# A two-layer hybrid backbone: who issues the stores of normalised tokens, and how many tiles of a SwiGLU begin with the first half

## The chip, the cores and the metric

One core of one Trainium2 chip. The metric is the device time of one execution in microseconds. Before the change it was 2889.73 us in the median of 3 runs (2886.65 to 2902.56).

## The reference

512 tokens of 1024 features go through two layers: 256 latent tokens and 256 context tokens. Each layer is a SwiGLU of half weight, a mixer of three branches (grouped attention, RWKV-7 and neighbourhood attention) and a second SwiGLU. Each of these three parts is modulated by a conditioning vector and closed by a layer norm:

```python
def post_norm(x, y, g, b):
    return layer_norm(ALPHA * x + y, g, b)

def swiglu(u, wi, wo):
    gate, up = jnp.split(u @ wi, 2, axis=-1)
    return (jax.nn.silu(gate) * up) @ wo

for l in range(DEPTH):
    x = post_norm(x, 0.5 * m_x[2] * swiglu(modulate(x, m_x[0], m_x[1]), ffn1_wi[l], ffn1_wo[l]), ...)
    ctx = post_norm(ctx, 0.5 * m_c[2] * swiglu(modulate(ctx, m_c[0], m_c[1]), ffn1_wi[l], ffn1_wo[l]), ...)
    y_x, y_c = hybrid_mixer(modulate(x, m_x[3], m_x[4]), modulate(ctx, m_c[3], m_c[4]), ...)
    x = post_norm(x, m_x[5] * y_x, ...)
    if not last:
        ctx = post_norm(ctx, m_c[5] * y_c, ...)
        ctx = post_norm(ctx, 0.5 * m_c[8] * swiglu(modulate(ctx, m_c[6], m_c[7]), ffn2_wi[l], ffn2_wo[l]), ...)
    x = post_norm(x, 0.5 * m_x[8] * swiglu(modulate(x, m_x[6], m_x[7]), ffn2_wi[l], ffn2_wo[l]), ...)
```

D_MODEL is 1024, D_FF is 2816, all in float32. In the last layer the context is dropped after the mixer's keys and values, so the last SwiGLU has latent tokens alone.

## The kernel before, in words

Everything lies transposed: features on the 128 partitions, tokens along a row of 512, of which the first 256 (`LAT`, "the first half") are latent tokens and the last 256 (`CTX`, "the second half") context. A D of 1024 is KD = 8 tiles, an FF of 2816 is KF = 22 tiles. A float32 product is made of three TensorE products: each operand is split into a high and a low part (`uh`/`ul` for the tokens, `whi`/`wlo` for a weight), and `gemm` adds high by high, high by low and low by high (L330 to L332).

A weight comes by `wload` (L307 to L325): SP issues a load into `raw` (L312; three buffers), ScalarE copies the high part (L320), VectorE subtracts (L321), which frees the buffer. High and low parts have two buffers each, unless the caller hands over tiles to hold them (`hold`): then a weight is split in two halves of 512 (`whh`/`whl` in a SwiGLU, `wG` in the mixer).

A SwiGLU (`ffn`, L462) runs over the 22 tiles of FF: a product with the gate weight (`ps_fg`), one with the up weight (`ps_fu`), silu on ScalarE into `sg` (L496), the product of the two on VectorE. Six banks are there for these products, two for each tile. Where both halves are present, the first `early` tiles are made by halves: first their products with the tokens of the first half, then those with the second half, since the second half's normalised tokens come later. The tiles from `early` on take all 512 tokens at once. Then follow eight output tiles (`ps_o`), the last of them by halves.

A layer norm stands between any two parts, for each half by itself. `ln_stats` (L408) makes the mean, the centred `z`, squares `sq` on ScalarE (L420), their sum on TensorE (`ps_ss`, L424), a small sum on VectorE, its power -1/2 on GpSimd (`rs`, L428), and spreads it on TensorE (`ps_bc`, L431). `ln_norm` (L434) multiplies z by it (L440) and modulates z into the next part's `uh`/`ul` (L351, L336, L337). In a second loop GpSimd applies gain and bias (`xn`, 128x256, L447, two buffers), and SP stores each xn in DRAM (`xd`, L450), from where the next part's residual reads it. Five norms have a next part, four of both halves and one of the first half alone: 72 stores of 128 KB. The sixth norm's eight stores are the output `out_y`.

The mixer begins with RWKV (`rwkv`, L903): four products of `ps_first` for both halves; the first two use weights that were split ahead (`ready`), the other two hold theirs in `wG` tiles. Their memory is where the SwiGLU's working tiles lay, xn among them. Behind them come gate products (`ps_gate`, L847 to L849) that fill gaps, and projections with weights of their own (L602, high part `phi`).

Each engine runs its instructions in one fixed order. A scheduler sets these orders when the kernel is built, by priorities and its own costs; SP's order is also that of its loads and stores. A transfer waits on the issuing engine for its data and for a free buffer, and what stands behind it there waits too.

Of the kernel before, what the change touches and what calls it, by code (L numbers as in the profile page):

```python
# [112 lines left out]
class Program:  # L113
# [320 lines left out]
    def ln_norm(self, l, ln, h, nxt, dst, bc, res=None):  # L434


        nc, z = self.nc, self.z
        for k in range(KD):
            with (self.tc.issue_after(res.ins) if res is not None and k >= 3 else nullcontext()):
                nc.vector.tensor_tensor(out=z[k][:, h], in0=z[k][:, h], in1=bc, op=ALU.mult)  # L440
                if nxt is not None:
                    self.modulate(k, h, z[k][:, h], *nxt)
        for k in range(KD):
            xn = self.tmp.tile([P, SEQ], F32, tag="xn", name="xn", bufs=2 if nxt is not None else 4)
            lg, lb = [self.lng[:, l, ln, i, k:k + 1] for i in range(2)]
            if nxt is not None:
                nc.gpsimd.tensor_scalar(out=xn, in0=z[k][:, h], scalar1=lg, scalar2=lb, op0=ALU.mult, op1=ALU.add)  # L447
            else:
                nc.scalar.activation(out=xn, in_=z[k][:, h], func=AF.Identity, scale=lg, bias=lb)
            nc.sync.dma_start(out=dst[k][:, h], in_=xn)  # L450

    def norm_dst(self, l, ln, nxt, final=None):
        if nxt is not None:
# [8 lines left out]
    def ffn(self, l, which, halves, nxt_fn, every, final=None, then=()):  # L462
        nc = self.nc
# [4 lines left out]
        with ExitStack() as ctx:  # L468
# [7 lines left out]
            two = len(halves) == 2  # L476
# [27 lines left out]
            def banks():  # L504
                return [self.bank("mm", [P, NT], n) for n in ("ps_fg", "ps_fu")]


            early = 2 if two else 0
            ps = [banks() for _ in range(early)]
            ready, self.ready = self.ready, []  # L510
            ws = [m == 0 and ready or load(m, True) for m in range(early)]
# [15 lines left out]
            nxt = nxt_fn()  # L527
            dst = self.norm_dst(l, ln, nxt, final)
# [1127 lines left out]
```

## Time and profile before

| | |
|---|---|
| runs | 2886.65, 2889.73, 2902.56 us |
| profiled execution, its own time | 2899.91 us |
| its span | 2898.1 us |
| granted TensorE clock, mean | 0.956 of full speed |
| busy, TensorE / VectorE / ScalarE / GpSimd | 2721.6 / 1715.2 / 1062.7 / 308.2 us |
| DMA | 379.74 MB in 207615 packets, none of them issued by GpSimd |

The busy times are those of one execution, and the span is the stretch that its trace covers; the 1.8 us around it are not in the trace. TensorE's granted clock is a share of its full speed: 2.4 GHz, with 1.2 GHz as the other level. In a timeline a row is one instruction, or several of a kind (xN), on an engine (PE is TensorE, DVE VectorE, ACT ScalarE, POOL GpSimd; SPq is SP's queue of DMA issues), with its start and its duration; brackets hold the engine's idle time before it and what ended that.

### The profile page before, as it was taken

The numbers are of one execution on the slowest core, as the hardware profiler recorded it, in microseconds if no ns is written. First come the engines' busy times: TensorE is split into PE (matmuls) and PEld (weight loads), VectorE is DVE, ScalarE is ACT, GpSimd is POOL, SyncE is SP. The second block draws the span as 40 slices with busy tenths as digits, with TensorE's granted clock in tenths as the row PEclk, the third lists the DMA queues.
The fourth block names the chain that finished last, engine by engine and source line by source line (L and its number), as shares of the span: only waits on it lengthen the run. The fifth ranks groups of instructions, "written<-read, shape, count | busy, mean of one in ns | idle before, by whom it ended". The sixth has DMA issues, their size and how long they took to land. (4 is left out here: it accounts for less than half of the span.)

```text
span 2898.1 us, 48420 instructions
## 1 busy us (share of the span) xinstructions
PE 2721.6 (94%) x19654; PEld 2218.8 (77%) x19654; DVE 1715.2 (59%) x2855; ACT 1062.7 (37%) x1928; POOL 308.2 (11%) x306
## 2 busy tenths in 40 slices
PE   7999998898899899999999999999898998898998
PEld 5788887676667676797888888888776777777998
DVE  4667345767652457657762476633578775386654
ACT  3222234333322346342222332322443443374443
POOL 0000022111100101220000100001221110022000
PEclk8999999999999999989999999999899999898998
DMA  7655342221133532436553465433332223544654
GB/s 281 203 179 176 105 126 92 76 70 48 53 89 119 153 114 87 146 117 197 178 164 108 126 200 181 135 102 116 112 114 64 62 71 101 164 129 143 218 178 146
DMA packets 207615, 379.74 MB, mean 131 GB/s; under 512 B 80032, under 2 KB 110368, under 8 KB 207392
## 3 DMA queue, kind: packets, MB, share of 16 engines
q1 hardware_dynamic: 207392, 376.65, 41.7%
q8 instruction: 154, 2.52, 0.4%
q14 instruction: 69, 0.57, 0.1%
HBM read 342.50 MB, written 33.03 MB: 130 GB/s over the span
## 5 line engine op out<-in xcount | busy, mean ns | idle before, releaser
L320 ACT ACTIVATE whi<-raw 128x1024 fp32r<-128x1024 f32 (+1 forms) x399 | 415.2, 1041 | 1117.6 <-PE ps_o L331 298.1
L321 DVE TENSOR_TENSOR wlo<-raw,whi 128x1024 fp32r<-128x1024 f32 (+1 forms) x399 | 499.2, 1252 | 499.1 <-ACT whi L320 493.0
L847 PE MATMUL ps_gate<-uh,whi 128*128 128x512 f32 (+1 forms) x672 | 266.8, 397 | 5.0 <-ACT fg L853 3.1
L330 PE MATMUL ps_o<-hh,whi 128*128 128x512 f32 (+1 forms) x770 | 270.8, 352 | 0.0
L253 DVE SCALAR_TENSOR_TENSOR acc<-araw,cs,acc 128x1024 f32<-128x1024 f32 x210 | 260.6, 1280 | 15.5 <-DMA araw<-in_w_ada 15.3
L332 PE MATMUL ps_o<-hh,wlo 128*128 128x512 f32 (+1 forms) x770 | 267.5, 347 | 0.0
L331 PE MATMUL ps_o<-hl,whi 128*128 128x512 f32 (+1 forms) x770 | 265.6, 345 | 0.0
L330 PE MATMUL ps_fg<-uh,whi 128*128 128x512 f32 (+1 forms) x704 | 256.3, 364 | 7.8 <-ACT uh L336 4.1
L332 PE MATMUL ps_fu<-uh,wlo 128*128 128x512 f32 (+1 forms) x704 | 252.8, 359 | 4.4 <-DVE wlo L321 4.4
L332 PE MATMUL ps_fg<-uh,wlo 128*128 128x512 f32 (+1 forms) x704 | 254.1, 361 | 2.3 <-DVE wlo L321 2.3
L331 PE MATMUL ps_fg<-ul,whi 128*128 128x512 f32 (+1 forms) x704 | 253.4, 360 | 0.1
L330 PE MATMUL ps_fu<-uh,whi 128*128 128x512 f32 (+1 forms) x704 | 251.9, 358 | 0.9 <-ACT whi L320 0.9
L331 PE MATMUL ps_fu<-ul,whi 128*128 128x512 f32 (+1 forms) x704 | 251.5, 357 | 0.0
L849 PE MATMUL ps_gate<-uh,wlo 128*128 128x512 f32 (+1 forms) x672 | 242.9, 361 | 1.1 <-DVE wlo L321 1.1
L848 PE MATMUL ps_gate<-ul,whi 128*128 128x512 f32 (+1 forms) x672 | 242.5, 361 | 0.0
L330 PEld LDWEIGHTS ps_fg<-uh,whi 128*128 128x128 f32 x704 | 135.4, 192 | 38.9 <-ACT whi L320 12.0
L332 PEld LDWEIGHTS ps_o<-hh,wlo 128*128 128x128 f32 x770 | 144.6, 188 | 20.2
L847 PEld LDWEIGHTS ps_gate<-uh,whi 128*128 128x128 f32 x672 | 131.6, 196 | 36.9 <-issue 7.2
L331 PEld LDWEIGHTS ps_o<-hl,whi 128*128 128x128 f32 x770 | 144.5, 188 | 19.5
L330 PEld LDWEIGHTS ps_o<-hh,whi 128*128 128x128 f32 x770 | 144.8, 188 | 19.0 <-ACT whi L320 1.7
L332 PEld LDWEIGHTS ps_fu<-uh,wlo 128*128 128x128 f32 x704 | 134.4, 191 | 26.0 <-DVE wlo L321 7.3
L332 PEld LDWEIGHTS ps_fg<-uh,wlo 128*128 128x128 f32 x704 | 135.1, 192 | 22.8 <-DVE wlo L321 3.3
(299 smaller groups left out, 5169.6 us busy)
## 6 DMA issues: line engine op xcount, KB each, us to landing
raw<-in_ffn_wi SPq DMA_DIRECT2D x176, 512.0 KB, 3.6
araw<-in_w_ada SPq DMA_DIRECT2D x144, 512.0 KB, 3.9
raw<-in_w_in SPq DMA_DIRECT2D x92, 512.0 KB, 3.6
raw<-in_ffn_wo SPq DMA_DIRECT2D x70, 448.0 KB, 3.3
raw<-in_ffn_wo SPq DMA_DIRECT2D x35, 512.0 KB, 3.5
pd<-fg SPq DMA_DIRECT2D x52, 256.0 KB, 2.0
raw<-in_w_branch SPq DMA_DIRECT2D x24, 512.0 KB, 3.8
raw<-in_w_in SPq DMA_DIRECT2D x44, 256.0 KB, 2.7
```

The lines of the kernel that those rows point to most:

```text
L253: nc.vector.scalar_tensor_tensor(out=a, in0=raw, scalar=c, in1=a, op0=ALU.mult, op1=ALU.add)
L320: nc.scalar.activation(out=hi[:, :m], in_=r, func=AF.Copy)
L321: self.lo = nc.vector.tensor_tensor(out=lo[:, :m], in0=r, in1=hi[:, :m].bitcast(F32), op=ALU.subtract)
L330: nc.tensor.matmul(pt, wh, xh[k], start=first and k == 0, stop=False)
L331: nc.tensor.matmul(pt, wh, xl[k], start=False, stop=False)
L332: nc.tensor.matmul(pt, wl, xh[k], start=False, stop=last and k == n - 1)
L847: nc.tensor.matmul(pt, wh, xh, start=k == 0, stop=False)
L848: nc.tensor.matmul(pt, wh, xl, start=False, stop=False)
L849: nc.tensor.matmul(pt, wl, xh, start=False, stop=k == KD - 1)
```

## The change

GpSimd issues the stores of xn where a next part follows; the output's stores stay on SP. A SwiGLU with two halves makes three tiles by halves instead of two, so the third tile's weights are held in split tiles too.

```diff
@@ ln_norm @@
             else:
                 nc.scalar.activation(out=xn, in_=z[k][:, h], func=AF.Identity, scale=lg, bias=lb)
-            nc.sync.dma_start(out=dst[k][:, h], in_=xn)
+            (nc.sync if nxt is None else nc.gpsimd).dma_start(out=dst[k][:, h], in_=xn)
@@ ffn @@
-            early = 2 if two else 0
+            early = 3 if two else 0
```

GpSimd's order from the first SwiGLU's norm to the mixer, before: the first half's xn, the second half's rs (`L428`), the second half's xn.

```order
L428 TENSOR_TENSOR rs<-rs,mhalf 128x2
L447 TENSOR_SCALAR xn<-z,c_lngb 128x256 x2
L908 MEMSET shp 128x2 x2
L1284 MEMSET R 128x256
L1285 MEMSET R 128x16
L447 TENSOR_SCALAR xn<-z,c_lngb 128x256 x6
L428 TENSOR_TENSOR rs<-rs,mhalf 128x2
L447 TENSOR_SCALAR xn<-z,c_lngb 128x256 x8
```

And now the end of the same stretch (the first half's last xn, and the first of the second half):

```order
L447 TENSOR_SCALAR xn<-z,c_lngb 128x256
L450 DMA xd_0_2334<-xn 128x256
L428 TENSOR_TENSOR rs<-rs,mhalf 128x2
L447 TENSOR_SCALAR xn<-z,c_lngb 128x256
L450 DMA xd_0_2334<-xn 128x256
```

Each of the 72 xn has its store right behind it, and the second half's rs comes behind eight xn and eight stores.

SP's order at the same place (`raw` are weights, those of L602 for the projections with `phi`; c_, lora and g_ are small constants):

```order
-L312 DMA raw<-in_w_in 128x1024 x3
-L450 DMA xd_0_2278<-xn 128x256 x2
-L312 DMA raw<-in_w_in 128x1024
-L450 DMA xd_0_2278<-xn 128x256 x2
+L312 DMA raw<-in_w_in 128x1024 x4
...
-L602 DMA raw<-in_w_in 128x512
-L450 DMA xd_0_2278<-xn 128x256 x2
-L1063 DMA g_4156<-in_lora 128x128
-L602 DMA raw<-in_w_in 128x512
-L450 DMA xd_0_2278<-xn 128x256 x4
-L312 DMA raw<-in_w_in 128x1024
-L450 DMA xd_0_2278<-xn 128x256 x4
-L312 DMA raw<-in_w_in 128x1024
```

All sixteen stores are gone from it; what stays are the loads, in their old order but for the small constants, which now stand ahead of both loads of L602.

TensorE's order at the end of this place, before: five gate products (`ps_gate`), then the first product with a held weight (`wG`).

```order
L847 MATMUL ps_gate_3638<-uh_2260,whi_3641 128x512
L848 MATMUL ps_gate_3638<-ul_2268,whi_3641 128x512
L849 MATMUL ps_gate_3638<-uh_2260,wlo_3642 128x512
L847 MATMUL ps_gate_3638<-uh_2261,whi_3641 128x512
L848 MATMUL ps_gate_3638<-ul_2269,whi_3641 128x512
L330 MATMUL ps_first_3380<-uh_2260,wG_3382 128x256
```

And now the last five of nine:

```order
L848 MATMUL ps_gate_3694<-ul_2325,whi_3697 128x512
L849 MATMUL ps_gate_3694<-uh_2317,wlo_3698 128x512
L847 MATMUL ps_gate_3694<-uh_2318,whi_3697 128x512
L848 MATMUL ps_gate_3694<-ul_2326,whi_3697 128x512
L849 MATMUL ps_gate_3694<-uh_2318,wlo_3698 128x512
L330 MATMUL ps_first_3436<-uh_2316,wG_3438 128x256
```

Four gate products have moved ahead of the first one with wG. On ScalarE phi stands behind two squares of the second half and ahead of six, where there were five and three.

## Rows read from the trace of the kernel before

**Rows 1.** Windows by stage; columns: stretch, length, busy us by engine, TensorE clock, DMA share, GB/s
```profile
400.00:480.00 80.00, 69.75 (x462) 63.14 (x462) 41.32 (x81) 38.46 (x75) 16.95 (x24) 0.91 0.37 113
1230.00:1290.00 60.00, 59.19 (x426) 57.83 (x426) 27.59 (x66) 25.50 (x57) 16.45 (x25) 0.86 0.26 82
2020.00:2090.00 70.00, 58.98 (x405) 55.06 (x404) 37.92 (x77) 34.36 (x70) 16.73 (x24) 0.85 0.37 117
```

**Rows 2.** Waits of SP's queue: line, releaser, us in total, times, longest us
```profile
SPq L450 <- POOL xn L447: 106.5, 54, 8.8
```

**Rows 3.** Tile xn: duration ns min/median/max; waits in us, times; landing us
```profile
L447 POOL TENSOR_SCALAR xn<-z,c_lngb x72: 552/556/1838, 425.6 to 2686.9; 128x256 f32<-128x256 f32 x72
L450 SPq DMA_DIRECT2D xd<-xn x72: 319/320/1299, 426.2 to 2687.4; - x72
...
  DMA xd<-xn: 29.2, 18
...
DMA to landing us min/median/max: 1.7/1.7/5.0
```

**Rows 4.** Lines of GpSimd by form: busy us, mean ns | idle before, releasers
```profile
L428 POOL TENSOR_TENSOR rs<-rs,mhalf 128x2 f32<-128x2 f32 x10 | 7.8, 781 | 95.3 <-DVE rs L427 95.3
```

**Rows 5.** Chain of waits, 2036 to 2080 us: start, duration, what
```profile
2063.54 1.45 POOL xn L447
...
2066.88 0.57 POOL xn L447
...
2072.38 1.72 DMA xd<-xn
```

**Rows 6.** Timeline of SP's queue at the first SwiGLU's norm: start, duration, instruction
```profile
435.40 0.37 SPq L602 DMA_DIRECT2D raw<-in_w_in  x1
```

**Rows 7.** Timeline of VectorE, same place
```profile
430.82 1.22 DVE L321 TENSOR_TENSOR wlo<-raw,whi 128x1024 fp32r<-128x1024 f32 x1
```

**Rows 8.** Timeline of ScalarE, same place; in brackets the idle time before, releaser
```profile
439.23 0.63 ACT L336 ACTIVATE phi<-raw 128x512 fp32r<-128x512 f32 x1 [3.18 <-DMA raw<-in_w_in]
...
459.57 1.67 ACT L320 ACTIVATE wG<-raw 128x512 fp32r<-128x512 f32 x3 [2.96 <-DMA xd<-xn]
```

**Rows 9.** Waits of TensorE, 420 to 480 us
```profile
PE ps_first L330 <- ACT wG L320: 2.4, 1, 2.4
PE ps_ss L424 <- ACT sq L420: 1.8, 1, 1.8
```

**Rows 10.** Timeline of GpSimd, 425 to 461 us
```profile
425.59 2.38 POOL L447 TENSOR_SCALAR xn<-z,c_lngb 128x256 f32<-128x256 f32 x2 [1.05 <-DVE z L440]
...
443.22 0.71 POOL L428 TENSOR_TENSOR rs<-rs,mhalf 128x2 f32<-128x2 f32 x1 [6.77 <-DVE rs L427]
445.29 1.09 POOL L447 TENSOR_SCALAR xn<-z,c_lngb 128x256 f32<-128x256 f32 x2 [1.37 <-DVE z L440]
```

**Rows 11.** Timeline of TensorE, 1289 to 1296 us: halves, then whole tiles
```profile
1289.80 0.28 PE L332 MATMUL ps_fu<-uh,whl 128*128 128x256 f32 x1
...
1292.04 0.40 PE L330 MATMUL ps_fg<-uh,whi 128*128 128x512 f32 x1
...
1295.92 0.39 PE L332 MATMUL ps_fg<-uh,wlo 128*128 128x512 f32 x1
```

**Rows 12.** Waits of TensorE, 2030 to 2090 us
```profile
PE ps_ss L424 <- ACT sq L420: 3.4, 1, 3.4
...
PE ps_first L330 <- ACT wG L320: 2.0, 1, 2.0
```

**Rows 13.** Timeline of GpSimd at the same norm of the second layer
```profile
2060.33 1.09 POOL L447 TENSOR_SCALAR xn<-z,c_lngb 128x256 f32<-128x256 f32 x2 [1.37 <-DVE z L440]
```

**Rows 14.** Timeline of ScalarE at the second layer's first SwiGLU
```profile
1654.95 0.63 ACT L320 ACTIVATE whh<-raw 128x512 fp32r<-128x512 f32 x1 [1.84 <-DMA raw<-in_ffn_wi]
```

**Rows 15.** Timeline of SP's queue at the last SwiGLU
```profile
2678.45 9.32 SPq L450 DMA_DIRECT2D xd<-xn  x8
```

**Rows 16.** Timeline of ScalarE at the last SwiGLU
```profile
2692.50 1.06 ACT L320 ACTIVATE whi<-raw 128x1024 fp32r<-128x1024 f32 x1 [1.39 <-PE ps_fg L331]
```

## The prediction

> **What bounds the kernel now.** I read the shares of busy time first (table above): TensorE is busy nearly all the time. A change that touches only GpSimd and SP can therefore pay only where TensorE stands still, so the second view is busy time by stage. Around the joints between a SwiGLU and the mixer TensorE is busy for 69.75 of 80 us and 58.98 of 70 us, at a granted clock of 0.91 and 0.85; at the joint from the first layer's mixer to its second SwiGLU it is busy for 59.19 of 60 us, so there is nearly nothing to win there [rows 1]. The third view is what SP's queue waits for: 54 of the 72 stores wait for their normalised token, 106.5 us in all [rows 2]. Every load queued behind such a store waits too, and that is what the move can free. The fourth view is the tile of normalised tokens, xn: GpSimd makes one in 0.56 us (median), at worst in 1.84 us; SP issues a store in 0.32 us and it lands after 1.7 us (medians); and GpSimd itself waits 29.2 us, 18 times, for a store to land, as there are two buffers [rows 3].
>
> **What moves.** All 72 stores of xn go from SP to GpSimd, where each stands behind its own xn; the eight stores of the final output stay on SP. GpSimd is not scarce, but its order is strict: between the first half's and the second half's tokens stands the rs of the second half's statistics, and it now stands behind eight issues more.
>
> **The unknown price c** is what one issue costs GpSimd. The trace has no transfer issued by GpSimd. From below it is SP's 0.32 us [rows 3]; from above I take 1.84 us, the slowest xn. Between them lies GpSimd's operation with next to no data, rs on 128x2, at 0.78 us mean [rows 4]. An issue touches no tile of data either, so it should stand near that row rather than at either end; I take 1.0 us, a little above it, and keep 0.32 and 1.84 for the range. The landing I leave at 1.7 us.
>
> With two buffers a round of two xn takes either xn, issue and landing (0.56 + c + 1.7), or two xn and two issues (1.12 + 2c), whichever is longer. At c = 1.0 that is 3.26 us. The round that binds today is 3.34 us (2063.54 to 2066.88 [rows 5]), so the rhythm stays. Eight tokens take three rounds, two xn with issue, and a landing: 3 x 3.26 + 3.12 + 1.7 = 14.6 us. At 0.32 it is 11.2 us, at 1.84 it is 20.9 us.
>
> By the Trainium skill ("DMA: Bandwidth & Descriptors", section "Anatomy of one DMA — SWDGE (gpsimd) path") a transfer issued by GpSimd takes about 2.0 us plus its bytes over 436 GB/s; for 128 KB that is an estimate of 2.3 us, where the SP-issued row has 1.7. By the page a group of eight would be four times 0.6 us longer, 2.4 us, and the sum below some 7 us higher, near 2893; no row of before can show it, and it stays inside no change.
>
> **Joint 1 (first SwiGLU to mixer, 425 to 462 us).** The load of a projection weight is issued at 435.40, behind stores, though its buffer was free at 430.82 + 1.22 = 432.04 [rows 6, 7]. ScalarE stands 3.18 us at phi for it, with three of the eight squares of the second half behind phi [rows 8], and TensorE waits 1.8 us for those squares [rows 9]. Without the stores the load goes out 3.4 us earlier. Phi moves ahead in ScalarE's order (behind two squares instead of five), so some of this stays; from the 1.8 us of TensorE and the 3.2 us of ScalarE I take 2.4. The rs is then at 440.8 instead of 443.22, and the first xn of this half at 442.9 instead of 445.29 [rows 10]. GpSimd is free for it: the first half's tokens begin at 425.59 and their last issue ends 14.6 - 1.7 later, at 438.5.
> The end of this joint is set by the last store: ScalarE's wG waits 2.96 us until it has landed, 459.57 [rows 8], and TensorE waits 2.4 us for wG [rows 9]. Now: 442.9 + 14.6 + 0.5 (half a chance of one xn slowed by 1.1 us) = 458.0, so 1.5 us earlier. Four more gate products stand ahead of the first product with wG, at 0.228 us each [rows 11], work that came after the wait: 0.9 us. Joint 1: **-2.4 us**.
>
> **Joint 2 (second layer, same code).** TensorE waits 3.4 us for squares here [rows 12]; I take 3.9 for the gain of the second half's chain, as the load is held longer. First xn of that half: 2060.3 [rows 13] - 3.9 = 2056.4; last landing 2056.4 + 15.1 = 2071.5 against 2072.38 + 1.72 = 2074.10 [rows 5]; with the gate products **-3.4 us**.
>
> **Starts of the SwiGLUs.** A tile's 48 products (gate and up, 8 tiles of D, three each) split into halves go from 0.228 us to two times 0.118 us (2.24 us for 19, 3.88 us for 17 [rows 11]): 48 x 0.008 = 0.36 us, in three SwiGLUs **+1.1 us**. What it would cover, a wait for the second half's norm, hardly exists: of 60 us 59.19 are busy [rows 1]. At the start of the second layer ScalarE stands 1.84 us at a held weight whose load left SP behind two stores [rows 14] and, behind it, the first half's modulation, for which TensorE waits. That load now leaves when its buffer is free, and no store holds the next ones: I count three quarters of the 1.84, **-1.4 us**. Three tiles take all six banks, so the fourth waits for the first tile's silu; that has the 11 us of the other two tiles' second half to finish in.
>
> **Joint 3 (last mixer to last SwiGLU, one half).** SP issues the eight stores in 9.32 us from 2678.45, one landing per round hidden by late tokens, and the last is down at about 2689.1 [rows 15]. On GpSimd, from an xn's 0.56 us before the first issue: 2677.9 + 14.6 = 2692.5, 3.4 us later. The first silu waits for it, and the third tile's weight split stands behind that silu with 1.39 us to spare [rows 16]: **+2.0 us**.
>
> Sum: -2.4 - 3.4 - 1.4 + 1.1 + 2.0 = **-4.1 us**, against the profiled execution's own 2899.9 us (span 2898.1). That execution lies 10 us over the median of the runs shown, 2889.73; the terms are differences, so I set them against the median: **2886 us**. A measurement of this kernel can tell about 0.5%, 14.5 us, from no change.
>
> **Rival one, slower: GpSimd is shut out while it issues.** The bound for it is in the trace: an xn takes 1.84 us in place of 0.56 when VectorE is at work beside it [rows 3]; one of 1.45 us stands in joint 2's chain [rows 5]. If every issue costs that, two xn and two issues are the round, 4.8 us, and eight tokens take 20.9 us. Joints 1, 2 and 3 end 6.3 us later each (+18.9). The first half's issues then last till 425.6 + 20.9 - 1.7 = 444.8 in joint 1, past the rs due at 440.8, and as far past it in joint 2: +4 to 5 us each. Two SwiGLU starts pass silu's deadline by some 3 us each. With the -4.1: about +30 us, **2919 us**. It decides from c = 1.2 us (sum zero) and is told from no change from about 1.5 us. For it speaks that VectorE is at work for half of joint 1's stretch, 41.32 of 80 us [rows 1]; against it, that the median of the 72 xn is at the low end, 0.56 us.
> The Trainium skill warns of this ("SBUF — State Buffer", the box "The 'DVE blocks DMA' trap (SWDGE)"): GpSimd writes the descriptors of its own transfers through a port shared with VectorE, and it advises SP's or ScalarE's queue instead. The same page's "Who interferes with whom" has two-operand operations bar only GpSimd's reads, by which the issue would be spared; the row shows reads barred and no issue.
>
> **Rival two, faster: the issue is as cheap as SP's.** At 0.32 us eight tokens take 11.2 us, and the stores cease to set the joints' ends. Then TensorE's own waits are the cap: 1.8 + 2.4 + 0.9 in joint 1 [rows 9], 3.4 + 2.0 + 0.9 in joint 2 [rows 12], joint 3 even, -1.8 at the second layer's start, +1.1: -12 us. With fewer stops the clock may also stay up: 9% of 80 us and 15% of 70 us, 17.7 us in all, are lost to it [rows 1]; a third of that is 6. **2872 us**.
>
> **Rival three, nothing happens:** the load that phi needs is bound by its buffer and the transfer, not by SP's queue, and the third tile covers a wait that isn't there. Then the eight tokens of joints 1 and 2 begin where they do now and end 0.9 and 1.3 us later, less 0.9 us of gate products each; with +1.1 and +2.0 that is about +3 us, **2893 us**.
>
> **Chances.** Forecast 0.40 and rival three 0.19 lie within 0.5%; rival one beyond 0.5% 0.23, for the price is unknown and the slope above 1.2 us is steep (some 4.6 us per tenth); rival two beyond 0.5% 0.18. The range goes from 2868 (rival two with a little more clock) to 2911 (rival one at about 1.65 us); some 0.06 lie below and 0.13 above.
>
> **What would show it.** Right: transfers of GpSimd in a queue of their own, about 1 us of GpSimd between one xn and the next, rounds of 3.3 us; phi's wait under 1.5 us, TensorE's wait for squares gone in both joints; wG released by the last store at 458 and 2071 plus the shift so far; the last SwiGLU's first silu 3 us later. Wrong: rounds of over 4 us, or a landing over 2.5 us; rs waiting behind the first half's issues; TensorE's waits for wG grown; or a granted clock that moves more than 0.01 over the span, which would outweigh every term here.

## The result and the profile after

The change makes the kernel slower: 2912.85 us in the median of 7 runs (2907.58 to 2916.63) against 2888.38 us before (7 runs as well, 2886.65 to 2902.56), a ratio of 1.0069 with a 95% interval of 1.0054 to 1.0084. The forecast was 2886 us with a range up to 2911. The profiled execution of the changed kernel took 2916.6 us (span 2914.9, mean granted clock 0.955), that of before 2899.9 (span 2898.1, 0.956); the two traces differ by 16.8 us, the medians by 24.5.

First the tile xn in the changed kernel (min/median/max in ns; waits in us, times; landing in us), which answers to [rows 3].

```profile
L447 POOL TENSOR_SCALAR xn<-z,c_lngb x72: 544/557/2670, 425.4 to 2704.7; 128x256 f32<-128x256 f32 x72
L450 POOL DMA_DIRECT2D xd<-xn x72: 587/587/747, 426.3 to 2705.5; - x72
...
  DMA xd<-xn: 11.8, 14
...
  ACT wG L320: 10.7, 2
...
  ACT L496: 7.1, 2
  ACT sg L496: 4.1, 1
...
DMA to landing us min/median/max: 1.7/2.1/5.3
```

An issue by GpSimd takes 0.59 us, nearly always the same, where SP's took 0.32. A store lands after 2.1 us where it took 1.7; both run from the start of the issue, and from its end the medians are 1.47 and 1.40 us, so most of the difference is the longer issue itself. GpSimd waits less for landings, 11.8 us instead of 29.2, but 42.8 us of issues now stand between its tokens. And what waits for the last store of a norm waits longer: wG 10.7 us in two places (5.5 before), silu, or the load of its table, in three SwiGLUs 11.2 us (0.9 in one before).

GpSimd's timeline in joint 1 shows what each token costs now; it answers to [rows 10].

```profile
425.43 0.56 POOL L447 TENSOR_SCALAR xn<-z,c_lngb 128x256 f32<-128x256 f32 x1 [1.05 <-DVE z L440]
...
430.21 0.59 POOL L450 DMA_DIRECT2D xd<-xn  x1 [0.30 <-POOL xn L447]
433.69 0.80 POOL L447 TENSOR_SCALAR xn<-z,c_lngb 128x256 f32<-128x256 f32 x1 [2.88 <-DMA xd<-xn]
...
441.49 0.59 POOL L450 DMA_DIRECT2D xd<-xn  x1 [0.30 <-POOL xn L447]
442.10 0.73 POOL L428 TENSOR_TENSOR rs<-rs,mhalf 128x2 f32<-128x2 f32 x1
444.14 0.56 POOL L447 TENSOR_SCALAR xn<-z,c_lngb 128x256 f32<-128x256 f32 x1 [1.31 <-DVE z L440]
...
458.40 0.59 POOL L450 DMA_DIRECT2D xd<-xn  x1 [0.30 <-POOL xn L447]
```

Behind each xn stand 0.30 us until its end is known, 0.59 us of issue and the next xn: 1.45 us at best. The first half's tokens run from 425.43 to 442.08; 2.88 us of that is a wait for a store of 428.18 that landed only after 5.3 us. And the second half's rs, which stands behind them, starts at 442.10, without a gap. The second half's tokens then take from 444.14 to 458.99. ScalarE's timeline at the same place ([rows 8] before):

```profile
435.42 0.64 ACT L336 ACTIVATE phi<-raw 128x512 fp32r<-128x512 f32 x1 [0.73 <-DMA raw<-in_w_in]
435.96 1.93 ACT L420 ACTIVATE sq<-z 128x256 f32<-128x256 f32 x6
...
460.62 0.63 ACT L320 ACTIVATE wG<-raw 128x512 fp32r<-128x512 f32 x1 [5.40 <-DMA xd<-xn]
```

Phi's wait has shrunk from 3.18 to 0.73 us and the eight squares are done at 437.9, as forecast. But the gain stops there: rs comes 4.2 us after the squares, and wG begins at 460.62, later than before (459.57). TensorE's waits, 420 to 480 us ([rows 9] before), say the same: the wait for squares is gone, one of 3.0 us for rs stands in its place, and the one for wG has grown from 2.4 to 4.0.

```profile
PE ps_first L330 <- ACT wG L320: 4.0, 1, 4.0
PE ps_bc L431 <- POOL rs L428: 3.5, 2, 3.0
```

The second loss is at the first layer's second SwiGLU. SP's queue there:

```profile
1301.35 0.81 SPq L242 DMA_DIRECT2D araw<-in_w_ada  x2
1302.27 0.37 SPq L312 DMA_DIRECT2D raw<-in_ffn_wi  x1
1306.49 0.33 SPq L242 DMA_DIRECT2D araw<-in_w_ada  x1
1306.87 0.90 SPq L356 DMA_DIRECT2D xr<-xd  x2
1309.47 17.78 SPq L242 DMA_DIRECT2D araw<-in_w_ada  x6
1328.10 0.33 SPq L312 DMA_DIRECT2D raw<-in_ffn_wi  x1
```

These araw are background work: weights of the next modulations, each load followed by 2.5 us of additions on VectorE (L253). Their first load waits until the last store of xn has landed and goes out at 1301.35, since its tile lies where xn lay. Then six more follow in a row, 17.78 us, before the fifth tile's second weight is loaded at 1328.10. What TensorE meets is on VectorE: the fourth tile's second `wlo` stands behind seven such pieces of additions, the first at 1305.05, and starts at 1326.82.

```profile
1326.82 1.22 DVE L321 TENSOR_TENSOR wlo<-raw,whi 128x1024 fp32r<-128x1024 f32 x1
```

The fifth tile's first `whi`, on ScalarE, stands behind a copy that waits for VectorE too. TensorE waits there as follows, first 1245 to 1350 us, then at the start of the second layer, 1640 to 1745 us, behind a product of the background itself.

```profile
PE ps_fu L332 <- DVE wlo L321: 4.3, 1, 4.3
PE ps_fg L330 <- ACT whi L320: 3.4, 1, 3.4
```

```profile
PE ps_ada L258 <- DVE acc L253: 7.7, 1, 7.7
```

At the last SwiGLU the first silu (with the load of its table) waits 5.84 us for the last store:

```profile
2707.89 1.28 ACT L496 ACT_TABLE_LOAD   x1 [5.84 <-DMA xd<-xn]
```

Busy time by stage answers to [rows 1]. The places are those of before, shifted by the lag so far: next to nothing was won where TensorE stood still.

```profile
400.00:480.00 80.00, 68.13 (x456) 62.08 (x455) 41.45 (x80) 38.03 (x75) 25.02 (x40) 0.89 0.35 114
1240.00:1300.00 60.00, 59.17 (x427) 57.80 (x426) 27.78 (x67) 23.48 (x57) 28.91 (x41) 0.86 0.28 93
2040.00:2110.00 70.00, 59.32 (x417) 54.72 (x417) 37.75 (x77) 35.65 (x72) 24.42 (x39) 0.90 0.36 117
```

How far each part is behind is seen from instructions that both traces have. The lag is the start in the changed kernel less that in the kernel before.

| instruction (start before) | changed | first part alone | second part alone |
|---|---|---|---|
| rs, first half, first norm (423.83) | -0.2 | -3.2 | -0.7 |
| first small rs of the mixer, L396 (481.69): end of joint 1 | +1.3 | -3.3 | +1.4 |
| rs, first half, mixer's norm (1250.68) | +10.2 | -1.2 | +5.8 |
| sixth silu of the second SwiGLU (1336.47) | +17.9 | +3.4 | +6.8 |
| rs, first half, its norm (1645.33) | +18.1 | +3.1 | +6.9 |
| sixth silu of the second layer (1730.05) | +18.9 | -1.7 | +7.4 |
| rs, first half, its norm (2037.25) | +18.9 | -1.7 | +7.4 |
| fifth shp of the mixer, L894 (2095.88): end of joint 2 | +16.3 | -4.2 | +6.3 |
| rs of the last mixer's norm (2675.78) | +13.4 | -5.8 | +9.0 |
| last rs (2888.78) | +16.5 | -2.2 | +6.5 |

Joint 1 costs 1.5 us, the second SwiGLU's start 7.7, the second layer's start 0.7, joint 2 gives 2.6, the last SwiGLU costs 3.1: 10.4 us of the 16.5. The rest lies in the mixers (+8.9 and -2.8). There the order of TensorE's instructions is that of before, and a second trace of the same changed kernel has +2.0 instead of +8.9 in the first mixer. The granted clock from 520 to 560 us is 1.00 before and 0.87 in the changed kernel, but 0.87 in that second trace too, so it doesn't tell the two apart. I count none of it for the change; what it is stays open.

A lag holds both waits and the granted clock. TensorE's idle time (the stretch between two rows of the table, less its busy time there) leaves the clock out, and shows the waits more plainly:

| TensorE idle, us | before | changed | second trace | first part alone | second part alone |
|---|---|---|---|---|---|
| joint 1 | 10.1 | 11.7 | 11.3 | 11.2 | 11.0 |
| second SwiGLU's start | 3.2 | 8.5 | 10.9 | 8.5 | 8.6 |
| second layer's start | 5.8 | 9.6 | 11.6 | 5.7 | 7.3 |
| joint 2 | 10.9 | 10.5 | 9.4 | 10.9 | 9.9 |
| last SwiGLU's start, to the fifth silu | 4.2 | 7.9 | 8.0 | 7.6 | 4.0 |

That is 14 us more than before in the changed kernel's trace and 17 in its second, of the 24.5 by which the medians differ; the rest is not placed. Joint 2 gave next to no waiting back: its 2.6 us are nearly all the same products at another clock.

```profile
2037.25:2095.88 58.63, 47.76 (x301) 43.76 (x300) 30.40 (x63) 30.40 (x62) 14.44 (x22) 0.83 0.31 97
2056.12:2112.13 56.01, 45.48 (x301) 41.24 (x300) 30.43 (x63) 30.25 (x63) 23.02 (x38) 0.88 0.31 102
```

The first row is from the kernel before, the second from the changed one; the columns are those of [rows 1].

### The profile page after: what moved, and what is told of

It reads as the page before. It is cut to its first block, busy times and chain, and to the rows that moved or that the text cites. A ratio compares the mean times of both kernels' runs of the same rounds, so it can differ in the third digit from the quotient of the medians.

```text
span 2914.9 us, 48751 instructions
## 1 busy us (share of the span) xinstructions
PE 2720.4 (93%) x19798; PEld 2218.4 (76%) x19798; DVE 1717.3 (59%) x2861; ACT 1062.6 (36%) x1934; POOL 355.2 (12%) x378
## 4 chain that ended last, share of the span: by engine, by line
PE 50%; DVE 6%; DMA 3%; issue 2%; ACT 2%; POOL 2%; SPq 0%; POOLq 0%; ACTq 0%; DVEq 0%
PE ps_o L330 3%; PE ps_o L332 3%; PE ps_o L331 3%; PE ps_fu L332 3%; PE ps_fu L330 3%; PE ps_fg L330 3%; PE ps_fu L331 3%; PE ps_fg L332 3%; PE ps_fg L331 3%; PE ps_gate L847 2%; PE ps_o L664 2%; PE ps_gate L848 1%; PE ps_gate L849 1%; PE ps_t L656 1%; PE ps_s L641 1%
## 5 line engine op out<-in xcount | busy, mean ns | idle before, releaser
L320 ACT ACTIVATE whi<-raw 128x1024 fp32r<-128x1024 f32 (+1 forms) x393 | 408.7, 1040 | 1087.3 <-PE ps_o L331 305.9
L321 DVE TENSOR_TENSOR wlo<-raw,whi 128x1024 fp32r<-128x1024 f32 (+1 forms) x393 | 491.3, 1250 | 497.4 <-ACT whi L320 491.5
L253 DVE SCALAR_TENSOR_TENSOR acc<-araw,cs,acc 128x1024 f32<-128x1024 f32 x210 | 260.4, 1278 | 22.1 <-DMA araw<-in_w_ada 21.9
L330 PE MATMUL ps_fg<-uh,whi 128*128 128x512 f32 (+1 forms) x680 | 247.0, 363 | 11.7 <-ACT whi L320 9.3
L332 PE MATMUL ps_fu<-uh,wlo 128*128 128x512 f32 (+1 forms) x680 | 243.3, 358 | 7.8 <-DVE wlo L321 7.8
L332 PE MATMUL ps_fg<-uh,wlo 128*128 128x512 f32 (+1 forms) x680 | 244.4, 359 | 1.2 <-DVE wlo L321 1.2
L331 PE MATMUL ps_fg<-ul,whi 128*128 128x512 f32 (+1 forms) x680 | 244.1, 359 | 0.1
L330 PE MATMUL ps_fu<-uh,whi 128*128 128x512 f32 (+1 forms) x680 | 242.5, 357 | 0.4 <-ACT whi L320 0.4
L331 PE MATMUL ps_fu<-ul,whi 128*128 128x512 f32 (+1 forms) x680 | 242.2, 356 | 0.0
L332 PEld LDWEIGHTS ps_fu<-uh,wlo 128*128 128x128 f32 x680 | 129.3, 190 | 28.3 <-DVE wlo L321 10.5
L849 PEld LDWEIGHTS ps_gate<-uh,wlo 128*128 128x128 f32 x672 | 131.9, 196 | 21.4 <-DVE wlo L321 2.2
```

The lines of the kernel that those rows point to most:

```text
L253: nc.vector.scalar_tensor_tensor(out=a, in0=raw, scalar=c, in1=a, op0=ALU.mult, op1=ALU.add)
L320: nc.scalar.activation(out=hi[:, :m], in_=r, func=AF.Copy)
L321: self.lo = nc.vector.tensor_tensor(out=lo[:, :m], in0=r, in1=hi[:, :m].bitcast(F32), op=ALU.subtract)
L330: nc.tensor.matmul(pt, wh, xh[k], start=first and k == 0, stop=False)
L331: nc.tensor.matmul(pt, wh, xl[k], start=False, stop=False)
L332: nc.tensor.matmul(pt, wl, xh[k], start=False, stop=last and k == n - 1)
```

## Experiments

**Which part costs?** Theory A blames the third tile's background work, theory B GpSimd's slower stores. First the two parts apart. The stores by GpSimd, two tiles by halves:

```diff
-            early = 3 if two else 0
+            early = 2 if two else 0
```

> Only the first part: GpSimd issues the stores, two tiles by halves as before. Theory A (the third tile by halves draws the background products of the modulation, their loads and VectorE work, ahead of the fourth tile's weights, and TensorE waits there): most of the loss is gone, 2886 to 2894 us, and TensorE's waits for whi and wlo at the first layer's second SwiGLU (7.7 us with the whole change) fall under 3 us. Theory B (an issue by GpSimd costs 0.9 us and lands after 2.1 us, so the last store of each norm is later and holds up silu and wG): the loss stays, 2905 to 2915 us.

Measured: 1.0019 (1.0004 to 1.0034). About a quarter of the loss; neither theory has all of it, and TensorE still waits 4.7 us for a `wlo` at the second SwiGLU, which theory A did not expect. The third tile with SP's stores:

```diff
-            early = 2 if two else 0
+            early = 3 if two else 0
```

> Only the second part: three tiles by halves, the stores on SP. Theory A: 2897 to 2910 us, with six loads of araw in a row ahead of the fourth tile's second weight and TensorE's waits for whi and wlo over 5 us there. Theory B: 2888 to 2892 us, the 1 us of the split products.

Measured: 1.0031 (1.0012 to 1.0051). The wait that theory A names is there, but TensorE meets it elsewhere in its order: behind a product of the background, which needs VectorE's additions (the profile puts the first of the two waits down to issue, the second to them). The lag hides most of it: 1.1 us at the second SwiGLU's start, where idle time is 5.4 us above that of before and the granted clock 0.96 instead of 0.93. TensorE's waits, 1245 to 1350 us and 1640 to 1745 us:

```profile
PE ps_ada L258 <- issue: 7.3, 1, 7.3
```

```profile
PE ps_ada L258 <- DVE acc L253: 4.7, 1, 4.7
```

The whole change with the background held back during the held loads, that of the second tile included, and made up for at the seventh and eighth tile:

```diff
-                    if next(slots) % every == 0:
-                        self.bg_after(1)
+                    if next(slots) % every == 0 and not held:
+                        self.bg_after(2 if two and 6 <= m < 8 else 1)
```

> The whole change, but the loads of the held weights bring no background piece (four pieces fewer before the fourth tile, made up at the seventh and eighth tile). Theory A: the waits for whi and wlo at the first layer's second SwiGLU fall from 7.7 us to under 3 us and the time to 2902 to 2907 us. Theory B: 2910 to 2915 us, as with the whole change.

Measured: 1.0015 (1.0000 to 1.0031), which is what the first part alone costs. The same edit with the stores on SP:

> Three tiles by halves with the stores on SP, the held loads bringing no background piece. Theory A (the pile of background pieces is all that the third tile costs): 1.000 to 1.001, where three tiles with the pieces measured 1.0031; TensorE's wait behind the background product (7.3 us at the first layer's second SwiGLU) gone. If the halves themselves or the third tile's held weights cost: 1.002 or more.

Measured: 1.0003 (0.9986 to 1.0020). The waits are gone; at the second layer's start these are left:

```profile
PE ps_fg L330 <- ACT uh L336: 1.0, 2, 0.6
PE ps_bc L431 <- POOL rs L428: 0.5, 1, 0.5
PE ps_fu L332 <- DVE wlo L321: 0.3, 1, 0.3
```

So the third tile by halves costs nothing that can be measured here, and gains nothing, once it brings no background work ahead of the fourth tile. No run has this edit with two tiles by halves, though: TensorE's idle time at the two SwiGLU starts, 0.7 and 1.9 us, is below that of the kernel before (3.2 and 5.8), so the edit may pay by itself and cover a small cost of the third tile. The changed kernel again, on the chip of the next three:

> The changed kernel itself, beside the next three on one chip. Both theories: 1.005 to 1.008 of the kernel before, as measured first.

Measured: 1.0092 (1.0070 to 1.0115). By this measurement the whole is more than its parts (0.19 and 0.31 points); by the first, 0.69, it can't be told from their sum. With GpSimd's later last store the background's first load is later too (1301.35, and 1295.12 with the second part alone), and seven pieces instead of two stand ahead of the fourth tile's second `wlo`. But TensorE's wait there is nearly the same (7.7 and 7.3 us), and the waits at the second layer's start differ by 3 us (7.7 and 4.7), so what makes the whole dearer is not shown.

**Does the memory that the last store holds cost?** Here xn lies in a pool at the end of the others, which wG, sg and araw don't take over (the mixer's pools have the same line):

```diff
+            self.xp = ctx.enter_context(self.tc.tile_pool(name=f"fx{l}{which}", bufs=2))
...
-            xn = self.tmp.tile([P, SEQ], F32, tag="xn", name="xn", bufs=2 if nxt is not None else 4)
+            xn = self.xp.tile([P, SEQ], F32, tag="xn", name="xn", bufs=2 if nxt is not None else 4)
```

> The whole change, with xn in memory of its own at the end of the pools, which the next part's first tiles (wG, silu's sg, the background's araw) do not take over; the stores are issued and land as before. Theory B (what the later last store costs comes through the memory that it holds): the waits of ScalarE for stores of xn (22 us in 5 places with the whole change) vanish, and the ratio falls by 0.3 to 0.5 points, to about 1.003. Theory A (what costs is only the count of background pieces ahead of the fourth tile): under 0.15 points.

Measured: 1.0084 (1.0060 to 1.0107), no gain over 1.0092. The waits didn't vanish but moved; who waited for xn in this kernel:

```profile
  ACT wG L320: 11.1, 2
...
  DVE acc L251: 9.5, 1
  ACT hh L336: 5.5, 1
...
  ACT whh L320: 5.1, 1
```

hh and whh wait for the store: the new place is taken over by other tiles early. wG starts at 455.29, before the last store of joint 1 has landed (459.02), and waits now for the last xn itself; so it seems to lie on the z that xn reads. Theory B as I had put it falls. The first part alone in this layout:

> The first part alone (stores by GpSimd, two tiles by halves) with xn in memory of its own. Theory B: 0.4 points under the first part alone (1.0019), so about 0.998. Theory A: within 0.15 points of it.

Measured: 1.0022 (1.0008 to 1.0036), and 1.0022 (1.0007 to 1.0037) when run again: no gain either. And SP's stores in this layout:

> The kernel before with xn in memory of its own, stores on SP. Theory B: only the two waits of wG (5.5 us) and the one of sg (0.9 us) go, the loads behind the stores stay late: 0.998 to 0.999. Theory A: 1.000.

Measured: 0.9941 (0.9921 to 0.9961), far better than expected, and repeated on another chip:

> The stores on SP with xn in memory of its own, once more, beside the others on this chip: 0.992 to 0.997 of before if the gain of 0.9941 holds.

Measured: 0.9960 (0.9942 to 0.9979). This is a version that beats both kernels, and it isolates the issuer: its source differs from that of the one before it only in who issues, and TensorE's order in joint 1 is the same. GpSimd and ScalarE in joint 1, stores by GpSimd:

```profile
438.36 0.59 POOL L450 DMA_DIRECT2D xd<-xn  x1 [0.30 <-POOL xn L447]
438.97 0.73 POOL L428 TENSOR_TENSOR rs<-rs,mhalf 128x2 f32<-128x2 f32 x1
441.08 0.56 POOL L447 TENSOR_SCALAR xn<-z,c_lngb 128x256 f32<-128x256 f32 x1 [1.38 <-DVE z L440]
...
453.37 0.55 POOL L447 TENSOR_SCALAR xn<-z,c_lngb 128x256 f32<-128x256 f32 x1
```

```profile
453.95 2.19 ACT L320 ACTIVATE wG<-raw 128x512 fp32r<-128x512 f32 x4 [5.53 <-POOL xn L447]
```

and stores by SP:

```profile
438.75 0.70 POOL L428 TENSOR_TENSOR rs<-rs,mhalf 128x2 f32<-128x2 f32 x1 [4.06 <-DVE rs L427]
440.88 1.09 POOL L447 TENSOR_SCALAR xn<-z,c_lngb 128x256 f32<-128x256 f32 x2 [1.44 <-DVE z L440]
...
449.58 0.56 POOL L447 TENSOR_SCALAR xn<-z,c_lngb 128x256 f32<-128x256 f32 x1 [0.38 <-POOL xn L447]
```

```profile
450.17 2.19 ACT L320 ACTIVATE wG<-raw 128x512 fp32r<-128x512 f32 x4 [1.80 <-POOL xn L447]
```

From the first xn of the second half to the last it takes 441.08 to 453.92 with GpSimd and 440.88 to 450.14 with SP: 12.8 against 9.3 us. With GpSimd rs stands right behind an issue; with SP, GpSimd has been idle for 4.06 us before it, waiting for its data alone.

**GpSimd's time or the transfer's path?** With SP's stores, each xn is made twice on GpSimd:

```diff
                 nc.gpsimd.tensor_scalar(out=xn, in0=z[k][:, h], scalar1=lg, scalar2=lb, op0=ALU.mult, op1=ALU.add)
+                nc.gpsimd.tensor_scalar(out=xn[:, 1:SEQ], in0=z[k][:, h][:, 1:SEQ], scalar1=lg, scalar2=lb, ...)
```

> Stores on SP, xn in memory of its own (0.996 of before, 0.9941 in another call), and GpSimd makes each xn twice, all columns but the first, which puts 0.56 us more GpSimd time on each token and leaves the store's path as it is. If GpSimd's time per token is what the moved stores cost: 0.56 of 0.89 us, so over half of the way from 0.995 to 1.0022, 0.998 to 1.001. If it is the path of the transfer (landing after 2.1 instead of 1.7 us): 0.994 to 0.997.

Measured: 1.0035 (1.0019 to 1.0050), more than expected and more than the loss that it was to explain. Each token has at least 0.57 us more on GpSimd, the landing is SP's:

```profile
L447 POOL TENSOR_SCALAR xn<-z,c_lngb x72: 548/555/2136, 425.1 to 2692.0; 128x256 f32<-128x256 f32 x72
L448 POOL TENSOR_SCALAR xn<-z,c_lngb x72: 567/570/1970, 425.8 to 2694.2; 128x255 f32<-128x255 f32 x72
...
DMA to landing us min/median/max: 1.7/1.7/3.8
```

So time on GpSimd between two tokens is enough to lose all of the gain. It isn't an exact copy of the issue: the second xn reads z once more beside VectorE (up to 1.97 us). GpSimd's stores with four buffers, where no token waits for a landing (`bufs=4`):

> Stores by GpSimd, two tiles by halves, xn in memory of its own with four buffers, so no token waits for a landing. If GpSimd's time per token costs: eight tokens still take 8 x 1.45 = 11.6 us and more beside VectorE, 1.000 to 1.002. If the landing costs: near the version with SP, 0.995 to 0.998.

> Stores by GpSimd with xn in memory of its own and two buffers, once more beside the other two: 1.001 to 1.004 of before.

Measured: 0.9992 (0.9977 to 1.0008), beside 1.0022 for two buffers on the same chip. So the landing has a share, 0.3 points; the other 0.3 to 0.5 points to SP's 0.994 to 0.996, measured on other chips, stay with four buffers. That they are GpSimd's time is what the xn made twice suggests. In the layout of before, four buffers:

> The first part with four buffers for xn instead of two, so GpSimd never waits for the store before last to land. Theory B: the eight tokens take 8 x 1.45 + 2.1 = 13.7 us from the first xn at most, some 2 us less than with two buffers where landings bind, so 2 to 5 us faster than the first part alone. Theory A: no difference over 2 us to the first part alone.

Measured: 1.0001 (0.9987 to 1.0015), against 1.0019: 0.18 points, some 5 us, at the upper end of the expected, though the intervals overlap. With SP's stores four buffers matter less:

> Stores on SP, xn in memory of its own, four buffers instead of two. If the landing of the store before last still binds the tokens: 2 to 4 us under the two-buffer version (0.9941 of before). If what that version gained is only that nothing waits for the last store: within 2 us of it.

Measured: 0.9945 (0.9924 to 0.9966), 3 us under two buffers on the same chip, inside both intervals: undecided.

**Where does GpSimd's issue pay?** GpSimd issues for the SwiGLUs' norms alone:

```diff
-            (nc.sync if nxt is None else nc.gpsimd).dma_start(out=dst[k][:, h], in_=xn)
+            (nc.sync if nxt is None or ln == 1 else nc.gpsimd).dma_start(out=dst[k][:, h], in_=xn)
```

> Two tiles by halves; GpSimd issues the stores of the SwiGLUs' norms alone, SP those of the two mixers' norms. If GpSimd's 0.9 us an issue costs where the second SwiGLUs start (with the first part alone +4.6 us and +5.7 us there) and pays elsewhere: 0.997 to 0.999 of before. If it costs everywhere alike: 1.001 to 1.002.

Measured: 0.9992 (0.9975 to 1.0008), 0.27 points or 8 us under the first part alone, though the two were measured on different chips and their intervals just touch. This points to the mixers' norms as the place where GpSimd's issue costs; at the SwiGLUs' norms it neither gains nor loses measurably. TensorE's idle time agrees at the last SwiGLU's start (4.2 us, as before, and 7.6 with the first part alone), but not at the second's (7.8 and 8.5, before 3.2), so for the first mixer it is not shown.

## Why the prediction was wrong

It missed in sign: no change to a little faster was forecast, +0.7% came, just above the range (2911). Slower by over 0.5% had 0.23. By parts: the stores were forecast at -5.2 us (-2.4 - 3.4 - 1.4 + 2.0) and cost 0.19 points alone, 5.5 us; the third tile was forecast at +1.1 us and cost 0.31 points alone, 9 us. Two steps failed, "GpSimd is free for it" and "What it would cover [...] hardly exists".

- **The price c was near** (1.0 forecast, 0.30 + 0.59 = 0.89 measured).
- **Joint 2 came near its number by luck.** -3.4 us was forecast, -2.6 came in the traces. But rs came 2.8 us earlier instead of 3.9, the eight tokens took 16.2 us to the last landing (2076.34 to 2092.55) instead of 15.1, and TensorE's waits for rs and wG grew by 3.0 us against the 3.4 for squares that went. Its idle time fell by 0.3 us; the other 2.3 are the same products at a granted clock of 0.88 instead of 0.83.
- **The length of eight tokens was mis-sized.** 14.6 us with the last landing was forecast, 15.1 with half of a slow xn; 14.85 + 1.45 = 16.3 came in joint 1 (444.14 to 458.99, landed at 460.44). The landing isn't what was too small: the sum puts 1.7 us behind the issue, where the row's 1.7 runs from its start, and behind GpSimd's issue it took 1.5. Too small was GpSimd's own part. The eight xn took 6.05 us instead of 8 x 0.56 = 4.5, and one waited 1.31 us for VectorE. The median hid this: the mean xn was 0.71 us in the trace of before (50.8 us for 72) and is 0.74 in the changed kernel (53.6).
- **"GpSimd is free for it" failed.** The first half's issues were to end at 438.5, 2.3 us ahead of the rs; they ended at 442.08. What the earlier load gave to the squares was thereby taken by rs, on the engine that the issues had been moved to. Joint 1 came out at +1.5 instead of -2.4.
- **The third tile was costed by its products alone** (+1.1 us, which the version with the background held back bears out as nothing measurable). The step that failed is "What it would cover [...] hardly exists", which stopped there: each held load issues a background piece, and so does each tile of the second half. Seven pieces instead of four, at 2.5 us of VectorE, now stood ahead of the first tile taken whole (the fourth, before it the third). TensorE waited 7.7 us for this at each of the two later SwiGLU starts. At the second layer's start, forecast at -1.4 us beside the products, the first part alone gained 4.8 us in its trace; the whole change lost 0.7. SP's order after the change has six such loads in a row at these starts; the prediction read it at joint 1 only.
- **Joint 3**: +2.0 forecast, +5.0 at the fifth silu there (from +13.4 to +18.4), of which 1.9 came back by the end. The direction and the place were right; the eight tokens were again too short.
- **Rival one** had the right sign and place for the wrong reason. GpSimd wasn't shut out: 72 issues took 587 to 747 ns, with VectorE at work beside them for two thirds of that time. The steady 0.89 us a token suffices, as the kernel with xn made twice suggests. By the Trainium skill ("SBUF — State Buffer", "Who interferes with whom") a VectorE instruction with two inputs in SBUF contends with GpSimd's reads, and the writing of descriptors isn't held up by it (the page calls this inferred). The trace agrees on both sides: beside such instructions xn stretched to 2.67 us, no issue over 0.75. The estimate from the Trainium skill ("DMA: Bandwidth & Descriptors", "Anatomy of one DMA — SWDGE (gpsimd) path"), 2.3 us for the transfer, is near the 2.1 of the trace.
- **Rival two's** condition, an issue as cheap as SP's, never held for GpSimd. That joints 1 and 2 have some 12 us to give was right all the same, as the version with SP's stores and xn apart shows: TensorE's idle time falls there from 10.1 and 10.9 us to 5.0 and 4.6 (5.1 and 5.2 in the second trace), 11 us in all. Its busy time for the same products falls by 6.7 us as well, at a granted clock of 0.90 and 0.89 instead of 0.88 and 0.83, near the 6 us that the rival gave to the clock.

## What to carry to other kernels

Moving a DMA issue to an engine that computes moves time into that engine's chain: cost it per item (the producer at its mean and not its median, the wait for it, issue, landing over buffers) and ask what stands behind the last item, not whether the engine is idle on average. When a loop bound or a prologue grows, list everything that its body emits, background work included, on every queue. And where the end of a phase is set by a store, look at which tiles take over its memory; putting the stored tile elsewhere gave here what the other issuer did not.

## What the runs showed of the hardware

A 128 KB store issued by GpSimd held that engine for 0.59 us, from 0.30 us after the end of the instruction that made its data, and landed after 2.0 to 2.1 us in the median; issued by SP it took 0.32 and 1.7 us. From the end of the issue the landing took 1.47 and 1.40 us. In the changed kernel 12 of GpSimd's 72 xn had no VectorE work beside them and took 0.55 us in the mean, the other 60 took 0.78; beside VectorE's splits of weights one took 2.67. An issue took up to 0.75 us where it mostly takes 0.59.
